# The gates and the second shift and scale of a diffusion layer: weighted sums of weight rows on the vector engine, with the matmul engine adding the 128 partial rows

## The chip, the cores and the metric

The kernel runs on one core of one Trainium2 chip. The engines are named as in the profile: PE is the matmul engine (PEld is its weight load, which overlaps its matmuls), DVE the vector engine, ACT the scalar engine, POOL GpSimd, SP the queue that issues most transfers. The metric is the device time of one execution in microseconds (us), the median of three runs; lower is better.

## The reference

The layer has adaLN modulation, two attentions in parallel (multi-head latent attention and 2-D neighbourhood attention over 512 latent and 256 context tokens), a gated residual, a router and 16 experts of which each token uses two. Only the first lines below are touched:

```python
def adaln(cond, w_mod, b_mod):
    return jnp.split(jax.nn.silu(cond) @ w_mod + b_mod, 6, axis=-1)
...
sh1, sc1, g1, sh2, sc2, g2 = [m[:, None, :] for m in adaln(c, w_mod[l], b_mod[l])]
hx = modulate(rmsnorm(x, norm_attn_g[l]), sh1, sc1)
...
x = x + g1 * mixed
hx2 = modulate(rmsnorm(x, norm_ffn_g[l]), sh2, sc2)
x = x + g2 * hierarchical_moe(hx2, ...)
```

`silu(c)` is one vector of 1024 numbers and `w_mod` is 1024 x 6144 in float32. The first 2048 columns (`sh1`, `sc1`) are wanted at once and are computed apart, early. The other 4096 columns (`g1`, `sh2`, `sc2`, `g2`) are one vector times 16 MB of weights, wanted only after the neighbourhood attention.

## The kernel before

All work is in float32, most of it as matmuls of a high and a low part: `mm3` issues three matmuls (lines 56, 57, 58), whose parts ACT (a copy to the short type) and DVE (the difference) make. The stages, in order of time: modulated norm and the projections (0 to 122 us); the neighbourhood attention (about 122 to 262 us); the latent attention (to about 390 us); output projection and router (to about 460 us); the experts and the last norm.

The change lies in the neighbourhood attention. Its loop (line 707) runs over 32 blocks: four pairs of heads, in each pair two heads of four row blocks. For a block, PE makes the scores (lines 599 and 600), DVE adds the bias (line 605, `na_max`) and takes the row maximum (line 469, `row_max`), ACT takes the exponentials (line 612), PE turns them (line 621, `na_turn`) one block later, and DVE and ACT in turn copy the turned block out (lines 81 and 83). Between these, PE projects the next pair's queries and keys (`na_project`, 24 `mm3` for a pair) or, in the last pair, the latent heads' values (`mla_values`); ACT and DVE split what PE made (lines 578 to 584) and the next pair's weights (lines 554 and 557). At a pair's end come the sums over values (line 630) and their normalisation (lines 479 to 490).

The four modulation vectors are computed in the same loop by `mod_rest` (line 509), called behind every second block, 16 times. Call n takes one tile of 128 rows of `w_mod` (k = n mod 8) and half of the columns (r = n // 8): two loads of 512 KB, then four matmuls with the 128 x 32 tile `sstat[:, k, :]` as the weights (column 0 is `silu(c)`, column 1 that of the context vector, the rest zeros) and 512 columns moving, each on its own 32 columns of PE (`tile_position`). The trace shows each of these float32 matmuls as two instructions, so eight for a call. Eight calls accumulate in one bank of the sums' memory; behind the eighth, DVE adds the bias row (line 524) and SP writes four rows of 512 to memory (line 525), from where `g1` (line 881), the router's weights (line 964), the second norm (lines 1069 and 1072) and `g2` (line 1331) read them.

The loads go by `load` (line 177) into tiles named `raw`, of which there are three. The same three tiles serve the weights of queries and keys (line 549, twice in a pair) and, in the last pair, seven loads for the latent attention (`mla_weights`, `mla_values`). All are issued in order on SP, and a load waits until its tile has been read to the end.

In this stage the order on each engine is written by a planner when the program is built: it goes by the program's order and its own estimates of durations, and lets later instructions go ahead of earlier ones that it takes to be not ready. On the chip each engine then keeps that order and waits where an operand is late. The experts' stage is ordered by hand.

Of the kernel before, what the change touches and what calls it, by code (L numbers as in the profile page):

```python
# [8 lines left out]
F32 = mybir.dt.float32  # L9
# [4 lines left out]
OP = mybir.AluOpType  # L14
# [3 lines left out]
P = 128  # L18
# [12 lines left out]
# columns of the constant pack  # L31
# [6 lines left out]
def hybrid_kernel(tc, nc, x_k, x_q, ctx, cvec, w_mod_a, w_mod_b, b_mod_c, b_mod_r, g_ffn_row,  # L38
# [25 lines left out]
    # low parts that wait for their turn on the vector engine  # L64
# [22 lines left out]
    def rstd_steps(out, ss, n, n_cols, wk, first=None):  # L87
        """1 / sqrt(ss / n + eps): the root of the scalar engine, and one Newton step on its inverse.
        Of a sum in two parts the first one comes earlier."""
# [25 lines left out]
    # ------------------------------------------------------------ constants and small parameters  # L115
# [31 lines left out]
    # ------------------------------------------------------------ pools of the first phases  # L147
# [4 lines left out]
    # the tokens come in the places of the attentions' results  # L152
# [12 lines left out]
    # the root's table, ahead of its use  # L165
# [35 lines left out]
    def bank(*nums):  # L201
        """A bank of the sums' memory, of those named in turn."""
        n = taken[nums] = taken.get(nums, -1) + 1
        return psA.tile([P, 512], F32, name="ps", tag=f"b{nums[n % len(nums)]}", bufs=1)
# [8 lines left out]
    # ------------------------------------------------------------ modulated norm of the tokens, channel-major  # L213
# [24 lines left out]
    def mod_sums(q):  # L238
        """Shift and scale of two channel tiles, for latent and context tokens."""
# [14 lines left out]
    def mod_first(c):  # L254
        """The same of one of the first two channel tiles."""
# [90 lines left out]
    # ------------------------------------------------------------ latents of keys and values, of queries  # L346
# [30 lines left out]
    # what leaves for the memory lies apart from what follows  # L377
# [49 lines left out]
    # ------------------------------------------------------------ ring of the experts' weights  # L427
# [17 lines left out]
    def load_experts(n, behind=None):  # L445
        """Starts the loads of the next n chunks of experts' weights, in the order of their use."""
        for i in range(len(loads), min(len(loads) + n, len(order))):
# [6 lines left out]
            # few in flight, so that the small transfers between them don't queue for long  # L454
# [7 lines left out]
    # ------------------------------------------------------------ neighbourhood attention  # L462
# [3 lines left out]
    def row_max(s):  # L466
        """A block's row maximum, negated."""
        nm = cst.tile([P, 1], F32, name="nm", tag="nm", bufs=8)
        ve.tensor_reduce(out=nm, in_=s, axis=AX.X, op=OP.max, negate=True)  # L469
        return nm  # L470

    def softmax_block(s, pr, ssum):
        """exp of a block of scores less their row maximum, and the row sums."""
        ac.activation(pr, s, AF.Exp, bias=row_max(s), accum_out=ssum)

    def normalise_steps(ssum, wk, hi, lo):
        """Divides a pair of heads' sums by their rows' sums, which are turned into rows on the way."""
# [21 lines left out]
    # the sums of the experts' rows, by tokens  # L499
# [4 lines left out]
    # the other modulations, as rows  # L504
    mod_d = tc.dram_tile([2, 4, 512], F32, name="mod_d")
    modf = mod_d.rearrange("r a b -> r (a b)")
    mod_ps = []

    def mod_rest(n):
        r, k = divmod(n, KT)  # L510
        if k == 0:
            br = nw.tile([P, 512], F32, name="br", tag="br", bufs=1)
# [3 lines left out]
            mod_ps[:] = bank(7), br, rows  # L516
        ps, br, rows = mod_ps
        ws = [load(w_mod_b[r, k, :, q * 1024:(q + 1) * 1024]) for q in range(2)]
        for g in range(4):
            pe.matmul(ps[g * 32:(g + 1) * 32, :], sstat[:, k, :],  # L520
                      ws[g // 2][:, g % 2 * 512:g % 2 * 512 + 512], start=(k == 0), stop=(k == KT - 1),
                      tile_position=(0, g * 32))
        if k == KT - 1:
            ve.tensor_tensor(br, br, ps, op=OP.add)
            sy.dma_start(mod_d[r], rows)
# [17 lines left out]
    def na_bias(p, u):  # L543
        """The bias of a head, with the window's mask."""
# [4 lines left out]
    def na_weights(p, j, i):  # L549
        """The high part (i = 0) and the low one (1) of the weights of queries (j = 0) or keys (1)."""  # L550
# [8 lines left out]
    def na_project(p, j):  # L559
        """Queries (j = 0), latent keys (1) or context's keys (2) of a pair of heads. Yields between the steps."""  # L560
# [9 lines left out]
    def na_part(p, j, u, i):  # L570
        """Their high part (i = 0) and low one (1), of a head."""
# [42 lines left out]
    def na_turn(p, u, i):  # L614
        """A block's weights by keys."""
# [32 lines left out]
    # ------------------------------------------------------------ latent attention  # L648
# [9 lines left out]
    def mla_values(t):  # L658
        """Values of the latent heads, and the queries' weights and latents in two parts. Yields between the steps."""
# [29 lines left out]
    for j in range(3):  # L689
        for n, _ in enumerate(na_project(0, j)):  # L690
# [4 lines left out]
            if n == 4 and j == 1:  # L695
                na_weights(1, 0, 0)
                na_weights(1, 0, 1)
                # the table of exp, ahead of its use
# [102 lines left out]
    def halves(n):  # L801
        """Two banks for sums of 1024 columns, by halves."""
# [11 lines left out]
    def k_rope(b):  # L814
        """The part of the keys that the heads share."""
        split_later(khs[b][64:96, :], kls[b][64:96, :], krt[64:96, :])

    def queries(a, ts=range(4)):
        """Queries of four heads."""
# [18 lines left out]
    def k_prep(p, hf):  # L838
        """Keys of a pair of heads, of the latent tokens (hf = 0) or the context's (1)."""
# [39 lines left out]
    # the neighbourhood heads' part of the output projection, between the pairs  # L879
# [55 lines left out]
    def mla_turn(h, t):  # L935
        """A block's weights by keys."""
# [22 lines left out]
    def router_weights():  # L959
        """The router's sums of the second shift, the same for all rows; then its weights take up the gains of the  # L960
# [937 lines left out]
```

## Time and profile before

| | |
|---|---|
| median of 3 runs | 760.02 us (759.91 to 760.87) |
| profiled execution, first to last instruction | 759.4 us |
| PE busy | 721.5 us, 95% of the span |
| DVE busy | 546.4 us, 72% |
| ACT busy | 446.0 us, 59% |
| mean granted TensorE clock | 0.980 |

The runs' median lies 0.6 us above the profiled span. Busy time is a sum over stages with different limits; a matmul's end is modelled in the profile, so how fast PE goes is better read from the starts of its instructions in order of time than from its busy share. A line such as "DVE L605 <- PE ps L600: 35.0" says that DVE stood idle for 35.0 us ahead of line 605 until line 600 on PE had ended.

### The profile page before, as it was taken

What the parts mean: (1) busy time and instruction counts of PE and PEld (TensorE: products, weight loads), DVE (VectorE), ACT (ScalarE), POOL (GpSimd) and SP (SyncE); (2) the same over time, 40 slices, a digit from 0 to 9 for tenths busy, and PEclk for the clock granted to TensorE, in tenths of its full rate; (3) what the DMA queues carried; (4) which work ended last, traced back from release to release, by engine and by line L of the source; (5) the groups of instructions that cost most, each with busy time, mean ns of one, the idle gap of its engine ahead of it and who ended that gap; (6) DMA issues with size and microseconds to landing.
All of it is one profiled execution on the core that took longest, in us unless ns stands there. A gap on an engine that the chain in (4) does not pass through costs nothing. (4 is left out here: it accounts for less than half of the span.)

```text
span 759.4 us, 10561 instructions
## 1 busy us (share of the span) xinstructions
PE 721.5 (95%) x3982; PEld 527.0 (69%) x3983; DVE 546.4 (72%) x744; ACT 446.0 (59%) x697; POOL 77.8 (10%) x46
## 2 busy tenths in 40 slices
PE   4999999999999999999999929999999999999995
PEld 4679987666665588776666826777777777777773
DVE  5572465646565589474564758999999999999996
ACT  6452364444434466464583428777777777777773
POOL 1000000000000000000000001033222322221220
PEclk9999999999999999999999958999999999999998
DMA  8931237544446662031139968999999999999872
GB/s 324 406 99 49 83 131 244 187 146 146 140 140 220 182 227 85 28 112 42 43 144 345 339 231 309 351 377 371 356 361 367 368 354 359 364 355 384 309 131 110
DMA packets 39621, 176.94 MB, mean 233 GB/s; under 512 B 5288, under 2 KB 6768, under 8 KB 27280
## 3 DMA queue, kind: packets, MB, share of 16 engines
q1 hardware_dynamic: 35168, 164.24, 58.6%
q0 software_dynamic: 4112, 11.92, 7.4%
q8 instruction: 32, 0.52, 0.3%
q14 instruction: 21, 0.17, 0.1%
q10 hardware_dynamic: 288, 0.08, 0.0%
HBM read 163.00 MB, written 15.32 MB: 235 GB/s over the span
## 5 line engine op out<-in xcount | busy, mean ns | idle before, releaser
L1356 DVE TENSOR_TENSOR el<-ew,eh 128x2048 fp32r<-128x2048 f32 (+1 forms) x106 | 220.5, 2087 | 20.7 <-ACT eh L1353 13.4
L1353 ACT CAST eh<-ew 128x1024 fp32r<-128x1024 f32 x190 | 189.7, 1048 | 43.2 <-PE s L58 28.6
L56 PE MATMUL s<-eh,xh 128*96 128x512 f32 x260 | 104.4, 401 | 0.9 <-ACT xh L61 0.9
L58 PE MATMUL s<-eh,xl 128*96 128x512 f32 x260 | 102.8, 396 | 0.0
L57 PE MATMUL s<-el,xh 128*96 128x512 f32 x260 | 102.4, 394 | 0.0
L1567 POOL DMA_INDIRECT ya_d<-yo,idx x14 | 45.5, 3253 | 140.4 <-DVE yo L1571 140.4
L58 PEld LDWEIGHTS s<-eh,xl 128*96 128x96 f32 x260 | 42.2, 162 | 19.1 <-DVE xl L62 0.6
L56 PEld LDWEIGHTS s<-eh,xh 128*96 128x96 f32 x260 | 42.2, 162 | 17.9 <-ACT xh L61 1.2
L57 PEld LDWEIGHTS s<-el,xh 128*96 128x96 f32 x260 | 42.3, 163 | 17.3 <-DVE el L1356 0.2
L56 PE MATMUL y<-eh,ghh 128*96 128x512 f32 x120 | 48.2, 401 | 0.0
L58 PE MATMUL y<-eh,ghl 128*96 128x512 f32 x120 | 47.3, 394 | 0.0
L57 PE MATMUL y<-el,ghh 128*96 128x512 f32 x120 | 47.2, 393 | 0.0
L56 PE MATMUL ps<-wh,hh 128*128 128x512 f32 (+2 forms) x128 | 43.8, 345 | 0.4 <-ACT hh L274 0.3
L469 DVE TENSOR_REDUCE nm<-s 128x1 f32<-128x768 f32 x32 | 30.5, 954 | 19.0 <-PE s L58 18.7
L58 PE MATMUL ps<-wh,hl 128*128 128x512 f32 (+2 forms) x128 | 43.5, 345 | 0.3 <-DVE hl L276 0.3
L57 PE MATMUL ps<-wl,hh 128*128 128x512 f32 (+2 forms) x128 | 43.3, 341 | 0.0
L1284 POOL MEMSET xg<- 128x1024 f32 x2 | 1.8, 950 | 388.0 <-DMA g<-mod_d 388.0
L605 DVE TENSOR_TENSOR ps<-ps,bb 128x256 f32<-128x256 f32 x32 | 13.8, 432 | 35.1 <-PE ps L600 35.0
L56 PE MATMUL ps<-hh,wh 128*128 128x512 f32 (+1 forms) x96 | 38.7, 403 | 0.0
L1242 POOL DMA_INDIRECT xg<-hx_d,idx x16 | 23.6, 1475 | 118.9 <-DVE va L1165 50.5
L933 ACT ACTIVATE pr<-s,nm 128x768 f32<-128x768 f32 x32 | 29.0, 908 | 9.6 <-DVE nm L469 9.3
L58 PE MATMUL ps<-hh,wl 128*128 128x512 f32 (+1 forms) x96 | 34.5, 359 | 0.0
(357 smaller groups left out, 1501.4 us busy)
## 6 DMA issues: line engine op xcount, KB each, us to landing
ew<-w_gate SPq DMA_DIRECT2D x32, 1024.0 KB, 9.3
ew<-w_up SPq DMA_DIRECT2D x32, 1024.0 KB, 9.2
ew<-w_down SPq DMA_DIRECT2D x32, 1024.0 KB, 9.3
raw<-w_mod_b SPq DMA_DIRECT2D x32, 512.0 KB, 3.8
wm<-w_mod_a SPq DMA_DIRECT2D x16, 512.0 KB, 9.2
raw<-w_qk SPq DMA_DIRECT2D x8, 512.0 KB
ya_d<-zero SPq DMA_DIRECT2D x10, 256.0 KB, 7.5
raw<-w_v SPq DMA_DIRECT2D x4, 512.0 KB
```

Source lines behind the costliest of these rows:

```text
L56: pe.matmul(ps, lh, rh, start=start, stop=False)
L57: pe.matmul(ps, lh, rl, start=False, stop=False)
L58: pe.matmul(ps, ll, rh, start=False, stop=stop)
L469: ve.tensor_reduce(out=nm, in_=s, axis=AX.X, op=OP.max, negate=True)
L605: ve.tensor_tensor(s[:, 0:256], s[:, 0:256], bb[:, 1 if i == 3 else 0, :], op=OP.add)
L933: ac.activation(pr, s, AF.Exp, bias=nm, accum_out=mla_ssum[h // 2][:, t, h % 2:h % 2 + 1])
L1242: ins = gp.indirect_dma_start(out=xg[e % NX][slice(0, CAP), :], out_offset=None, in_=hx_d, in_offset=bass.IndirectOffsetOnAxis(ap=idx[slic ...
L1284: gp.memset(x_, 0.0)
L1353: ac.copy(wh[:, cs], r[:, cs])
L1356: ve.tensor_tensor(wl[:, cs], r[:, cs], f(wh[:, cs]), op=OP.subtract)
L1567: gp.indirect_dma_start(out=ya_d, out_offset=bass.IndirectOffsetOnAxis(ap=idx[rows, 1, e:e + 1], axis=0), in_=yo[rows, :], in_offset=None, ...
```

## The change

`mod_rest` is rewritten, and the layout of its weights with it. The columns are now taken in eight pieces of 512 (r = n // 2), and each piece is finished by two calls, each of which takes four of the eight row tiles. For each row tile DVE multiplies the tile's 128 x 512 weights by `silu(c)` of the row (a scalar for each partition) and adds them to `macc`, a 128 x 512 tile. Behind the eighth row tile PE multiplies a 128 x 32 tile of ones by `macc`, 128 columns on each of its four strips, which adds the 128 rows; DVE adds the bias and SP writes a row of 512, eight times instead of two rows of 2048. The bytes loaded and the number and size of these loads (32 of 512 KB) are the same.

```diff
-    mod_d = tc.dram_tile([2, 4, 512], F32, name="mod_d")
-    modf = mod_d.rearrange("r a b -> r (a b)")
+    mod_d = tc.dram_tile([8, 4, P], F32, name="mod_d")
+    modf = mod_d.rearrange("(h r) a b -> h (r a b)", h=2)
     mod_ps = []
+    macc = nw.tile([P, 512], F32, name="macc")
+    ones = nw.tile([P, 32], F32, name="ones")
+    ve.memset(ones, 1.0)
 
     def mod_rest(n):
-        r, k = divmod(n, KT)
-        if k == 0:
-            br = nw.tile([P, 512], F32, name="br", tag="br", bufs=1)
+        r, h = divmod(n, 2)
+        if h == 0:
+            br = nw.tile([P, P], F32, name="br", tag="br", bufs=1)
             ve.memset(br, 0.0)
             rows = br.rearrange("(a b) n -> a b n", b=32)[:, 0, :]
             sy.dma_start(rows, b_mod_r[r])
-            mod_ps[:] = bank(7), br, rows
-        ps, br, rows = mod_ps
-        ws = [load(w_mod_b[r, k, :, q * 1024:(q + 1) * 1024]) for q in range(2)]
-        for g in range(4):
-            pe.matmul(ps[g * 32:(g + 1) * 32, :], sstat[:, k, :],
-                      ws[g // 2][:, g % 2 * 512:g % 2 * 512 + 512], start=(k == 0), stop=(k == KT - 1),
-                      tile_position=(0, g * 32))
-        if k == KT - 1:
-            ve.tensor_tensor(br, br, ps, op=OP.add)
+            mod_ps[:] = br, rows
+        br, rows = mod_ps
+        for k2 in (2 * h, 2 * h + 1):
+            w = load(w_mod_b[r, k2])
+            for i in range(2):
+                k = 2 * k2 + i
+                wk = w[:, i * 512:i * 512 + 512]
+                if k == 0:
+                    ve.tensor_scalar(macc, wk, sstat[:, k, 0:1], None, op0=OP.mult)
+                else:
+                    ve.scalar_tensor_tensor(macc, wk, sstat[:, k, 0:1], macc, op0=OP.mult, op1=OP.add)
+        if h:
+            ps = bank(7)
+            for g in range(4):
+                pe.matmul(ps[g * 32:(g + 1) * 32, 0:P], ones, macc[:, g * P:(g + 1) * P], start=True, stop=True,
+                          tile_position=(0, g * 32))
+            ve.tensor_tensor(br, br, ps[:, 0:P], op=OP.add)
             sy.dma_start(mod_d[r], rows)
...
-    a["w_mod_b"] = c(wm[:, 2048:].reshape(KT, P, 2, 2048).transpose(2, 0, 1, 3))
+    a["w_mod_b"] = c(wm[:, 2048:].reshape(4, 2, P, 8, 512).transpose(3, 0, 2, 1, 4).reshape(8, 4, P, 1024))
...
-    a["b_mod_r"] = c(bm[2048:].reshape(2, 4, 512))
+    a["b_mod_r"] = c(bm[2048:].reshape(8, 4, P))
```

## Rows read from the trace of the kernel before

**Rows 1.** Busy us by stretch, four pairs of heads: PE, PEld, DVE, ACT, POOL; clock, DMA

```profile
122.00:155.30 33.30, 33.30 (x172) 21.63 (x171) 19.60 (x35) 13.94 (x31) 0.00 (x0) 1.00 0.57 180
155.30:191.80 36.50, 36.50 (x213) 24.07 (x214) 20.22 (x36) 16.23 (x33) 0.00 (x0) 1.00 0.45 152
191.80:227.50 35.70, 35.70 (x208) 23.19 (x208) 19.99 (x36) 15.53 (x33) 0.00 (x0) 1.00 0.42 135
227.50:262.00 34.50, 34.50 (x182) 19.20 (x182) 20.24 (x36) 17.61 (x37) 0.00 (x0) 1.00 0.59 197
```

**Rows 2.** Waits in 122 to 262 us: total, times, longest

```profile
PEld ps L599 <- DVE pt L81: 0.8, 1, 0.8
```

**Rows 3.** PE in order of time, around one call and where none is; the group

```profile
134.91 0.60 PE L621 MATMUL ps<-c,pr 128*128 128x128 f32 x4
135.44 1.06 PE L520 MATMUL ps<-raw,sstat 128*32 128x512 f32 x8
136.44 0.50 PE L56 MATMUL ps<-hh,wh 128*128 128x512 f32 x1
...
176.29 0.60 PE L621 MATMUL ps<-c,pr 128*128 128x128 f32 x4
176.65 0.48 PE L56 MATMUL ps<-hh,wh 128*128 128x512 f32 x1
...
L520 PE MATMUL ps<-raw,sstat 128*32 128x512 f32 x128 | 20.2, 605 | 0.0
```

**Rows 4.** PE in order of time, a call in two parts

```profile
240.30 1.05 PE L520 MATMUL ps<-raw,sstat 128*32 128x512 f32 x4
241.29 0.50 PE L56 MATMUL ps<-wh,kvh 128*128 128x512 f32 x1
```

**Rows 5.** PE in order of time, 128-column matmuls of the first modulations

```profile
25.19 1.52 PE L245 MATMUL ps<-wm,sstat 128*32 128x128 f32 x48
...
42.39 0.42 PE L245 MATMUL ps<-wm,sstat 128*32 128x128 f32 x6
42.74 0.50 PE L56 MATMUL ps<-wh,hh 128*128 128x512 f32 x1
```

**Rows 6.** DVE groups by shape, 0 to 120 us: busy us, mean ns

```profile
L275 DVE SCALAR_TENSOR_TENSOR xnt<-xnt,ab,hh 128x576 f32<-128x576 f32 x8 | 6.4, 814 | 1.9 <-ACT hh L274 1.9
L276 DVE TENSOR_SCALAR hl<-xnt,ab 128x576 fp32r<-128x576 f32 x8 | 4.0, 515 | 0.1
L275 DVE SCALAR_TENSOR_TENSOR xnt<-xnt,ab,hh 128x256 f32<-128x256 f32 x8 | 3.8, 479 | 0.7 <-ACT hh L274 0.7
L276 DVE TENSOR_SCALAR hl<-xnt,ab 128x256 fp32r<-128x256 f32 x8 | 2.7, 349 | 0.1
```

**Rows 7.** DVE in order of time: a dependent pair, then two independent ones

```profile
126.19 0.43 DVE L605 TENSOR_TENSOR ps<-ps,bb 128x256 f32<-128x256 f32 x1 [1.05 <-PE ps L600]
126.66 1.29 DVE L469 TENSOR_REDUCE nm<-ps 128x1 f32<-128x512 f32 x2
```

**Rows 8.** DVE groups by shape, 122 to 290 us: the small steps

```profile
L833 DVE TENSOR_TENSOR q<-s,ckq 128x128 f32<-128x128 f32 x8 | 2.3, 286 | 0.7 <-ACT qt L832 0.7
...
L524 DVE TENSOR_TENSOR br<-br,ps 128x512 f32<-128x512 f32 x2 | 1.4, 689 | 1.7 <-PE ps L520 1.7
...
L513 DVE MEMSET br<- 128x512 f32 x1 | 0.5, 485 | 0.1
```

**Rows 9.** Busy us by stretch, in the experts' stage

```profile
520.00:700.00 180.00, 180.00 (x856) 128.02 (x855) 170.04 (x103) 138.52 (x154) 46.29 (x19) 1.00 1.02 364
```

**Rows 10.** DVE in order of time, end of the stage

```profile
259.81 0.69 DVE L524 TENSOR_TENSOR br<-br,ps 128x512 f32<-128x512 f32 x1 [1.43 <-PE ps L520]
260.42 0.68 DVE L81 COPY pt<-ps 128x512 f32<-128x512 f32 x1
```

**Rows 11.** SP's waits, 122 to 262 us; transfers issued 225 to 262 us

```profile
SPq L179 <- PE ps L520: 73.5, 19, 8.3
...
raw<-w_mod_b SPq DMA_DIRECT2D x8, 512.0 KB, 3.9
```

## The prediction

> **What bounds the kernel now.** I read the busy time by stretch first, then the waits, then PE in order of time. The change touches one stage, 122 to 262 us. [...] A busy PE alone proves little, since its ends are modelled; the waits say more. The longest time for which PE's weight load waited for another engine in these 140 us is one wait of 0.8 us [rows 2]. So PE sets the pace here, and a microsecond less on PE is one less of the stage as long as nothing else is late. DVE has 140 - 80.05 = 60 us of gaps (sum of the four stretches [rows 1]). What follows the stage hangs on it as a chain: the latent attention begins when the tiles and sums of this stage are given back, and the experts' loads begin behind it. I let it move by what the stage gains or loses, and keep 1 us either way for it in the range.
>
> **What is taken from PE.** One call shows as eight instructions of 605 ns, which does not mean 4.8 us: the four strips run side by side. From the turn ahead of it (134.91) to the matmul behind it (136.44) pass 1.53 us, and where no call stands between a turn and that matmul, 0.36 us (176.29 to 176.65); a call costs 1.17 us of PE [rows 3]. Thirteen of the sixteen calls are whole. The last three, all in the last pair, are cut in two because their two loads land apart, and each half costs 0.99 us (240.30 to 241.29), as much as a whole call less the change of tile [rows 4]. The group's 20.2 us busy are 19 pieces of 1.06 us, which agrees: 13 + 6 [rows 3]. Removed: 13 x 1.17 + 6 x 0.99 = 21.1 us; by pairs 4.7, 4.7, 4.7 and 7.1.
>
> **What PE gets instead.** Eight groups of four matmuls over 128 columns, two instructions each. The first modulations have the same form: in a long run 48 instructions take 1.52 us, so eight take 0.25 us; a short group of six takes 0.35 us from its start to the next matmul [rows 5]. I take 0.5 us, with bounds of 0.25 and the 0.99 of a half call [rows 4]: 4.0 us, 1.0 in each pair. PE then needs 33.3 - 3.7 = 29.6, 36.5 - 3.7 = 32.8, 35.7 - 3.7 = 32.0 and 34.5 - 6.1 = 28.4 us.
>
> **What DVE gets.** 64 new steps on 128 x 512: 56 multiply-adds with a scalar for each partition and 8 plain multiplications. Both forms stand in the first stage with 576 and 256 columns; between them, 512 columns make 479 + (814 - 479) x 256/320 = 747 ns and 349 + (515 - 349) x 256/320 = 482 ns [rows 6]. How far apart they start depends on whether they hang on one another: the maximum that reads what line 605 wrote starts 0.47 us after it, 0.04 more than it took; of two independent steps of 0.69 us the two together take 1.29, so they start 0.60 apart, 0.08 less than one takes [rows 7]. All eight sums of a piece hang on one another through `macc`, but other steps may stand between. Bounds: all dependent, 56 x 0.787 + 8 x 0.522 = 48.3 us; all hidden, 56 x 0.667 + 8 x 0.402 = 40.6 us. Neither row is nearer, since the planner will use part of the seams; I take the middle, 44.4. The small steps: eight adds of 128 columns at 0.286 for two of 0.689, +0.9 us; eight memsets of a quarter of the columns, at most 0.2 each, for two of 0.485, +0.6 at most, say +0.4 [rows 8]. Together 45.7 us, 11.4 in each pair.
>
> **The sum.** DVE then needs 31.0, 31.6, 31.4 and 31.6 us in the four pairs, against 29.6, 32.8, 32.0 and 28.4 on PE. So the two stand level, and in the first and last pair DVE is the longer. With both filled to the last gap the stage would take 31.0 + 32.8 + 32.0 + 31.6 = 127.4 us, 12.6 less. That will not happen: DVE keeps its order and has to wait for scores, exponentials and loads. The nearest stretch in which DVE is nearly full beside a PE that never stops is the experts', 170.04 of 180 us, a fill of 0.945 [rows 9]. At that fill the pairs take 32.8, 33.4, 33.2 and 33.4, 132.8 us, which is 7.2 less. The end of the stage gives some back: the last call's four sums, the ones and the add now stand where one add of 0.69 us stood, ahead of a copy that the last turn waits with [rows 10]. That is between nothing, if the sums are done while PE still projects, and 3 us, the four sums in a row; I take 1.5. Net 5.7 us less on the profiled span: 759.4 - 5.7 = 753.7, and with the 0.6 us by which the median lies above it 754.3 us.
>
> Edits that I cost at nothing: the loads are the same in number and size; six more writes of 2 KB and six more small loads of the bias go through SP, which in this stage waits 73.5 us for PE to give back the `raw` tiles [rows 11], so its own issue time is covered; the new rows are read only after the stage, and their writes are spread over it. If that cover were gone, a write or a load of the bias would delay the `raw` load behind it by its issue alone. New on DVE is a wait for loads. Before, the loads were PE's operands; now everything behind a sum in DVE's order (bias, maximum, then ACT's exponentials, then PE's turn) waits with it.
>
> [...] The rows give 0.47 us from start to start for a dependent pair whose first takes 0.43, and 0.60 for two independent ones of 0.69 [rows 7]. [...]
>
> **The rivals.**
> *DVE's chain is cheap.* If dependent sums start as close as independent ones, the added work is 40.6 + 1.3 = 41.9 us, 10.5 a pair, and DVE's pairs at the same fill take 31.9, 32.5, 32.3 and 32.5. PE's 32.8 counts in the second, so 129.5 us; with the 1.5 of the end, 9.0 less: 751.0 us. For it: other steps that stand between two sums hide the seam. Against it: four sums come at a time and hang on one another.
> *Everything packs.* 12.6 less and no loss at the end: 747.4 us. Against it: no stretch of the trace has DVE at 1.00.
> *The gain is eaten.* All sums at the dependent price: 49.6 us, 12.4 a pair, 32.0, 32.6, 32.4 and 32.6, at the fill of 0.945 together 137.2; with 3 us at the end the stage is as long as before, 760.2 us.
> *Slower: the three `raw` tiles hold the last pair.* There, 15 loads pass through three tiles (8 of the modulations [rows 11], 7 of the latent attention). A tile is held from its load's issue to its last reader: 3.9 us to land [rows 11], two sums (1.5 us), and the time for which it waits in DVE's order. The ring takes 15/3 = 5 holds, so it stays inside the pair's 33.4 us while a hold is under 6.7 us, a wait of 1.3 us. If each load waits behind a burst of four sums and one more step, 3.6 us, the hold is 9.0 and the pair takes 45 us where it took 34.5. Some loads are read by ACT and released earlier; with half of this excess the pair takes 39.2, the stage 138.6 and the end up to 3 us: 141.6, 1.6 slower; with all of it 144.4 + 3, 7.4 slower. I put it at the middle, 4.5 slower: 764.5 us. For it: the loads of this pair are late even now (the cut calls [rows 4]). Against it: the planner can place sums later when it sees the load late.
>
> **How the numbers follow.** Forecast 754.3 us with 0.45; the cheap chain 0.14; everything packs 0.06; eaten 0.12; slower 0.23. A measurement of this kernel can tell some 0.2%, 1.5 us, from no change. The first three are faster by more than that: 0.65; the fourth is the same: 0.12; the fifth slower: 0.23. The range for 8 in 10 reaches from everything packed, 747, to just under the slower rival's point, 764. The forecast's own range, with 0.25 to 0.99 us for the ones and 0 to 3 us at the end, is 751 to 758.
>
> **What would show it.** Right: line 520's successor on PE takes under 5 us in all; DVE is over 90% busy from 122 us to the stage's end; that end comes 4 to 8 us earlier; PE shows waits of about a microsecond for exponentials or for `macc`; the stages behind keep their lengths. The price of a sum is read from its row: 0.75 us each, 0.67 to 0.79 from start to start. Wrong: if DVE stays under 85% busy while PE waits, it is the order or the loads that hold, not DVE's work; if SP's waits for sums grow and ACT or DVE wait for `raw` in the last pair, it is the ring. If the stage's end moves and the kernel's does not, the later stages are not the plain chain that I take them for.

## The result, and the profile after

The changed kernel takes 764.97 us (median of 14 runs, 761.32 to 767.26) where the kernel before takes 759.79 on the same chip (14 runs, 757.49 to 761.76): a ratio of 1.0066, 95% interval 1.0051 to 1.0082. It is 5.2 us slower, where 5.7 us less were forecast, and 1 us above the range. The profiled execution went from 759.4 to 765.0 us and the mean granted clock from 0.980 to 0.960.

How long the touched stage takes is best read between two matmuls that stand in both kernels with the same work between them: the first projection of queries (`ps<-hh,wh`) and the first matmul of the latent attention (`o<-kvh,wkh`). Before they start at 104.06 and 265.24 us, after at 103.06 and 272.17: 161.2 and 169.1 us. From there to the end of the span pass 494.2 and 492.8 us. So the stage lost 7.9 us in these two executions and the stages behind kept their length. The change's profiled execution took 767.18 us, 2.2 more than its median, and its clock of 0.960 is the lowest of its 14 runs (median 0.967); the one of the kernel before took 759.91. So 7.9 us is more than the change costs in the middle. This stage length is used for all kernels below. (Some expectations quote how far the change stood ahead at the ends of the pairs, 3.7, 2.0, 0.7 and then 6.9 us behind, counted from the start of the span. The first projection itself starts up to 3 us apart in these executions; counted from there it is 2.7, 1.0, then 0.3 and 7.9 behind.)

The same stretches as [rows 1], and the rest of the stage, in the changed kernel (PE, PEld, DVE, ACT, POOL; clock, DMA):

```profile
122.00:155.30 33.30, 33.30 (x196) 24.09 (x194) 27.19 (x51) 15.16 (x33) 0.00 (x0) 1.00 0.61 199
155.30:191.80 36.50, 36.50 (x198) 25.81 (x192) 29.98 (x55) 16.00 (x33) 0.00 (x0) 1.00 0.45 153
191.80:227.50 35.70, 33.26 (x177) 22.38 (x175) 29.24 (x54) 15.05 (x32) 0.00 (x0) 0.90 0.42 137
227.50:262.00 34.50, 31.53 (x133) 19.49 (x129) 26.57 (x47) 13.97 (x30) 0.00 (x0) 0.75 0.53 171
262.00:272.20 10.20, 7.96 (x55) 5.66 (x55) 3.05 (x6) 2.59 (x6) 0.00 (x0) 0.67 0.52 175
```

The third column from the right is the news: the clock is granted in full for 70 us, then 0.90, 0.75 and 0.67 of it. DVE is fuller than before, but is busy for only 116.03 of these 150.2 us, and PE has gaps that it did not have. The waits of PE from 104 to 272 us (total, times, longest); in the kernel before PE has none to the stage's end at 265.24 us ([rows 2] shows its weight load, PEld):

```profile
PE ps L634 <- ACT pr L625: 2.2, 2, 1.4
PE ps L535 <- DVE macc L531: 2.1, 2, 1.2
PE ps L612 <- ACT pr L625: 1.7, 1, 1.7
PE ps L58 <- DVE wl L570: 1.2, 1, 1.2
PE ps L56 <- ACT wh L567: 0.5, 1, 0.5
```

Seven waits, 7.7 us. The groups that the change brought (line, engine, operation, tiles, shapes and count; busy, mean ns of one; idle before), DVE's four and PE's one:

```profile
L531 DVE SCALAR_TENSOR_TENSOR macc<-raw,sstat,macc 128x512 f32<-128x512 f32 x56 | 41.2, 735 | 0.1
L529 DVE TENSOR_SCALAR macc<-raw,sstat 128x512 f32<-128x512 f32 x8 | 3.7, 462 | 0.0
L537 DVE TENSOR_TENSOR br<-br,ps 128x128 f32<-128x128 f32 x8 | 2.3, 286 | 9.9 <-PE ps L535 9.9
L518 DVE MEMSET br<- 128x128 f32 x8 | 1.3, 165 | 0.0
...
L535 PE MATMUL ps<-macc,ones 128*32 128x128 f32 x64 | 3.9, 319 | 2.1 <-DVE macc L531 2.1
```

The prices are those of the forecast: 735 ns for a sum (747 from [rows 6]), 462 for a product (482), 0.49 us of PE for the ones (0.5). What the forecast has no line for is the 9.9 us that DVE stood ahead of the eight adds, until PE came to the ones.

**How a PE wait comes about.** DVE from the bias of one block (L618 at 233.15) to its row maximum (L469 at 240.38); columns are start, duration, line, operation, tiles:

```profile
233.15 0.43 DVE L618 TENSOR_TENSOR ps<-ps,bb 128x256 f32<-128x256 f32 x1 [1.24 <-PE ps L613]
233.49 0.68 DVE L62 TENSOR_TENSOR wl<-raw,wh 128x512 fp32r<-128x512 f32 x1
...
234.69 0.48 DVE L529 TENSOR_SCALAR macc<-raw,sstat 128x512 f32<-128x512 f32 x1
...
235.69 0.74 DVE L531 SCALAR_TENSOR_TENSOR macc<-raw,sstat,macc 128x512 f32<-128x512 f32 x1
...
236.49 0.73 DVE L531 SCALAR_TENSOR_TENSOR macc<-raw,sstat,macc 128x512 f32<-128x512 f32 x1
237.13 0.68 DVE L488 TENSOR_TENSOR rsb<-ps,rsb 128x512 f32<-128x512 f32 x1
237.73 0.74 DVE L531 SCALAR_TENSOR_TENSOR macc<-raw,sstat,macc 128x512 f32<-128x512 f32 x1
238.90 0.96 DVE L62 TENSOR_TENSOR uq<-raw,uq 128x768 fp32r<-128x768 f32 x1 [0.42 <-ACT uq L61]
239.78 0.68 DVE L490 TENSOR_TENSOR onl<-rsb,onh 128x512 fp32r<-128x512 f32 x1
240.38 0.68 DVE L469 TENSOR_REDUCE nm<-ps 128x1 f32<-128x512 f32 x1
```

The bias and the maximum that belong together stand 7.2 us apart. In the kernel before they are never more than 1.2 us apart in the last pair (2.0 in the whole stage); one of its blocks:

```profile
237.64 0.42 DVE L605 TENSOR_TENSOR ps<-ps,bb 128x256 f32<-128x256 f32 x1
...
238.84 0.68 DVE L469 TENSOR_REDUCE nm<-ps 128x1 f32<-128x512 f32 x1
```

Between the two steps of the changed kernel stand four steps of the sums, and copies and splits. ACT waits for that maximum, and PE for ACT's exponentials:

```profile
241.10 0.69 ACT L625 ACTIVATE pr<-ps,nm 128x512 f32<-128x512 f32 x1 [1.71 <-DVE nm L469]
...
241.93 0.38 PE L612 MATMUL ps<-kk,qh 128*128 128x256 f32 x1 [1.66 <-ACT pr L625]
```

**What comes behind it.** The stretches around PE's waits (the clock is the third number from the right):

```profile
200.00:210.00 10.00, 8.83 (x34) 6.49 (x34) 8.34 (x15) 4.83 (x11) 0.00 (x0) 0.83 0.46 146
220.00:230.00 10.00, 9.19 (x53) 5.33 (x51) 7.13 (x13) 4.72 (x10) 0.00 (x0) 0.83 0.69 222
240.00:245.00 5.00, 3.35 (x13) 1.96 (x11) 4.67 (x9) 2.39 (x5) 0.00 (x0) 0.86 0.49 168
245.00:260.00 15.00, 14.10 (x42) 8.40 (x42) 12.45 (x23) 5.03 (x11) 0.00 (x0) 0.50 0.60 194
260.00:265.00 5.00, 2.36 (x16) 1.66 (x18) 3.22 (x6) 2.78 (x6) 0.00 (x0) 0.84 0.23 77
265.00:270.00 5.00, 5.00 (x40) 3.79 (x42) 1.53 (x4) 0.62 (x1) 0.00 (x0) 0.50 0.78 245
```

From 245 to 260 us the granted clock is 0.50 without a break: matmuls of 512 columns start 0.43 us apart (256.98 to 257.41), where at 1.00 they start 0.23 us apart (237.12 to 237.35). The value sums of the last pair, 4.03 us long before (260.86), take 6.33 us here (265.49). Summed over these stretches, (1 - clock) x length is 1.7 + 1.7 + 0.7 + 7.5 + 0.8 + 2.5 = 14.9 us of matmul time not granted. The 2.2 us behind them, at a clock of 0.79, add 0.5. The sum is an upper bound of the cost, since PE also stood in some of this time.

**What no wait shows.** PE's new order also makes its own work longer. In the kernel before, the sums over values of the second pair stand in one run of 40:

```profile
192.94 3.72 PE L630 MATMUL ps<-pt,nav 128*64 128x512 f32 x40
```

In the changed kernel they stand in three pieces, one of two matmuls at 178.76 us and these, with the ones between them:

```profile
189.99 3.30 PE L643 MATMUL ps<-pt,nav 128*64 128x512 f32 x36
...
193.58 1.07 PE L643 MATMUL ps<-pt,nav 128*64 128x512 f32 x2
```

A piece of two takes a microsecond by itself and less than 0.2 within a run. From each piece's start to the start of what follows it, the value sums of the first three pairs take 11.9 us in 4 pieces before. In e4 (below), which issues the same 10 pieces for them as the change, they take 15.9 at the full clock and with no wait among them: 4.0 us more.

### The profile page after: what moved, and what is told of

Read it like the earlier page. It is cut to its first block, busy times and chain, and to the rows that moved or that the text cites. A ratio compares the mean times of both kernels' runs of the same rounds, so it can differ in the third digit from the quotient of the medians.

```text
span 765.0 us, 10562 instructions
## 1 busy us (share of the span) xinstructions
PE 720.5 (94%) x3918; PEld 533.3 (70%) x3919; DVE 584.4 (76%) x821; ACT 445.5 (58%) x697; POOL 77.7 (10%) x46
## 4 chain that ended last, share of the span: by engine, by line
PE 88%; DVE 5%; ACT 3%; DMA 3%; issue 1%; SPq 0%; DVEq 0%; ACTq 0%
PE s L56 11%; PE s L58 11%; PE s L57 11%; PE ps L56 6%; PE ps L58 6%; PE ps L57 6%; PE y L58 4%; PE y L56 4%; PE y L57 4%; PE ps L643 3%; PE o L968 3%; PE tr L959 3%; PE ps L613 2%; PE ps L634 2%; PE ps L612 2%; PE t L1511 1%
## 5 line engine op out<-in xcount | busy, mean ns | idle before, releaser
L469 DVE TENSOR_REDUCE nm<-s 128x1 f32<-128x768 f32 x32 | 30.5, 954 | 18.9 <-PE s L58 18.6
L531 DVE SCALAR_TENSOR_TENSOR macc<-raw,sstat,macc 128x512 f32<-128x512 f32 x56 | 41.2, 735 | 0.1
L625 ACT ACTIVATE pr<-ps,nm 128x512 f32<-128x512 f32 x32 | 22.0, 689 | 28.7 <-DVE nm L469 28.6
```

Of the source, the lines that this page charges most:

```text
L531: ve.scalar_tensor_tensor(macc, wk, sstat[:, k, 0:1], macc, op0=OP.mult, op1=OP.add)
```

## The experiments

All times are compared with runs of the kernel before on the same chip (medians 759.4 to 760.5). The kernels ran on several chips, so a difference of two of these medians is good to about a microsecond. "Pieces" are the eight of 512 columns, two to a pair of heads. Stage lengths come from one profiled execution each, from the first projection to the first latent matmul as above; that execution's own time stands beside them. The planner plans every kernel anew, so an edit can change the order on DVE and PE beyond its own lines.

| kernel | pieces on DVE | median us | ratio to before (95%) | profiled us | stage us |
|---|---|---|---|---|---|
| before | none, old layout | 759.79 | | 759.91 | 161.2 |
| the change | 0 to 7 | 764.97 | 1.0066 (1.0051 to 1.0082) | 767.18 | 169.1 |
| e1_late_add | 0 to 7, add one call later | 763.12 | 1.0040 (1.0016 to 1.0064) | 766.15 | 166.3 |
| e2_no_loads | 0 to 7, no loads for 6 and 7 | 761.40 | 1.0016 (0.9996 to 1.0036) | 761.25 | 164.8 |
| e3_filler | 0 to 7, matmuls added | 761.99 | 1.0031 (1.0015 to 1.0047) | 762.82 | 165.8 |
| e10_short_sums | 0 to 7, 6 and 7 of 64 columns | 755.08 | 0.9943 (0.9924 to 0.9961) | 753.48 | 156.5 |
| e7_pe_as_written | 0 to 7, PE's order as written | 782.87 | 1.0303 (1.0267 to 1.0340) | 782.80 | 183.3 |
| e6_only_last_dve | 6, 7 | 764.91 | 1.0052 (1.0026 to 1.0079) | 761.06 | 162.6 |
| e4_last_pe | 0 to 5 | 754.97 | 0.9924 (0.9900 to 0.9947) | 758.66 | 154.3 |
| e12_last_pe_late_add | 0 to 5, add one call later | 755.62 | 0.9944 (0.9926 to 0.9961) | 761.98 | 159.5 |
| e5_alt_pe | 0, 2, 4, 6 | 755.64 | 0.9950 (0.9927 to 0.9972) | 753.80 | 156.3 |
| e11_first_two_dve | 0 to 3 | 752.72 | 0.9917 (0.9891 to 0.9942) | 750.33 | 153.6 |
| e9_135_67_pe | 0, 2, 4 | 752.35 | 0.9887 (0.9852 to 0.9922) | 752.29 | 153.1 |
| e13_all_pe | none, new layout | 756.92 | 0.9973 (0.9960 to 0.9987) | 754.55 | 158.7 |

Many of the profiled executions lie far from their kernel's median, e6, e11 and e13 below it, e1, e4 and e12 above it. From the stage's end to the end of the span pass 492.2 to 494.9 us in all of them but e4 (498.3) and e12 (496.4); what these two took longer lies in part behind the stage.

Four theories stood at the start. The handshake: DVE stands 9.9 us ahead of the adds. DVE's queue: in the last pair bias and maximum come too late. The ring: the loads wait for one of three `raw` tiles, the slower rival of the prediction. The clock: PE's waits are short (1.7 us at most), but after them the granted clock is lower, 0.50 from 245 to 260 us.

**Put the add off (handshake).** The sum of the ones stays in its bank until the next call:

```diff
-            br = nw.tile([P, P], F32, name="br", tag="br", bufs=1)
+            br = nw.tile([P, P], F32, name="br", tag="br", bufs=2)
...
-            ve.tensor_tensor(br, br, ps[:, 0:P], op=OP.add)
-            sy.dma_start(mod_d[r], rows)
+            closing.append((br, rows, ps, r))
+        elif closing:
+            mod_close()
```

> The add of a piece's bias (line 537) and the write behind it are put one call later, eight times, so that the vector engine no longer stands before it until the matmul engine has come to the ones; all other work is the same. Theory A (the handshake between the two engines starts the loss: the vector engine stood 9.9 us before these adds, 3.3 us at each pair's end): the end of the attention stage, seen in the first matmuls behind the last transposed normalisation, comes from 271.8 us back to 262 to 266 and the kernel takes 755 to 759 us. Theory B (the vector engine is simply too full in the last pair): 762 to 766 us. Theory C (the three raw tiles): 762 to 766 us.

Measured: 763.12 us. The wait only moved. What DVE waited for from 104 to 272 us in this kernel (total, times, longest):

```profile
DVE macc L529 <- PE ps L535: 4.7, 3, 3.3
DVE rsb L488 <- PE ps L651: 4.3, 1, 4.3
DVE br L545 <- PE ps L535: 4.0, 1, 4.0
```

One of the first line's instances, in order of time:

```profile
193.49 0.48 DVE L529 TENSOR_SCALAR macc<-raw,sstat 128x512 f32<-128x512 f32 x1 [3.28 <-PE ps L535]
```

There is one `macc`, so the next piece's first product may not overwrite it before the ones have read it: the same PE instruction, the same 3.3 us. A second run of this edit without sums in the last pair (e12, below) gained nothing either. Taking the wait away altogether, with two `macc` tiles, was not tried.

**Take the loads of the last pair away (ring).** Pieces 6 and 7 read a tile that is there anyway, so they are not computed from their weights; all instructions of DVE and PE remain.

```diff
-            w = load(w_mod_b[r, k2])
+            w = load(w_mod_b[r, k2]) if r < 6 else nav[:, 2 * (k2 % 3):2 * (k2 % 3) + 2, :].rearrange("p a b -> p (a b)")
```

> In the last pair of heads the four calls make no loads: their sums read a tile that has lain in SBUF for long, so this part of the computation is left out in its meaning but not in its work on the vector and matmul engines. Theory C (three raw tiles hold the last pair, 15 loads through three of them): with 7 loads left the pair is free of them and the kernel takes 754 to 758 us. Theory B (the vector engine's work there): 762 to 766 us, since all sums are still made. Theory A (the handshake): 762 to 766 us.

Measured: 761.40 us, 3.6 less than the change, between the two ranges, and still not faster than before. The ring has a share; it is not the whole.

**Shorten the sums of the last pair, keep the loads (DVE's queue against the ring).** All loads, tiles, ones and writes stay; for pieces 6 and 7 only the first 64 columns are summed, the others are left out.

```diff
+                cols = 64 if r > 5 else 512
-                wk = w[:, i * 512:i * 512 + 512]
+                wk = w[:, i * 512:i * 512 + cols]
+                ma = macc[:, 0:cols]
```

> The changed kernel with the sums of the last pair (pieces 6 and 7) cut from 512 to 64 columns; the loads, their size, their tiles, the ones and the writes stay. The sums of the other columns of these two pieces are left out. The vector engine has some 16 x 0.6 = 10 us less to do in the last pair, the ring of raw tiles holds as many loads as before. If the vector engine's time is what makes this pair late, the pair takes what it takes with the sums on the matmul engine or less, and the time is 752 to 757 us. If the loads that wait for a tile make it late, little is gained: 761 to 765 us.

Measured: 755.08 us, 9.9 less than the change. Together with the run before it this shows which of the two leads. The ring carries as many loads as in the change, yet the whole loss of the last pair is gone (e4, below, has no sums there and takes as long). Short sums also give their tiles back sooner, so this run alone would not part the two; but with these loads out of the ring and the sums in full length (e2) 6.3 of the 9.9 us are still there. SP's longest wait for a sum to give a tile back, from 225 to 266 us, is 4.2 us in the change (total, times, longest):

```profile
SPq L179 <- DVE macc L531: 10.2, 6, 4.2
```

and here 1.2 us for a sum (L533), and 3.5 for a product (L531), once, at the pair's start:

```profile
SPq L179 <- DVE macc L533: 5.5, 8, 1.2
...
SPq L179 <- DVE macc L531: 3.5, 1, 3.5
```

So SP's waits alone don't tell DVE's queue and the ring apart; the times of e2 and e10 do.

**Only the last pair, and all but the last pair.** Pieces not on DVE are multiplied on PE in the new layout, four matmuls of 128 columns for each row tile; here for e4, with the list 0 to 5 for e6:

```diff
+        if r in (6, 7):
+            ps = mod_ps[2]
+            for k2 in (2 * h, 2 * h + 1):
+                w = load(w_mod_b[r, k2])
+                for i in range(2):
+                    k = 2 * k2 + i
+                    for g in range(4):
+                        o = i * 512 + g * P
+                        pe.matmul(ps[g * 32:(g + 1) * 32, 0:P], sstat[:, k, :], w[:, o:o + P],
+                                  start=(k == 0), stop=(k == KT - 1), tile_position=(0, g * 32))
```

> Pieces 0 to 5 (the first three pairs of heads) are summed on the vector engine as in the change; pieces 6 and 7 (the last pair) are multiplied and added on the matmul engine, four matmuls of 128 columns on each row tile. In the changed kernel the stage stood 3.7, 2.0 and 0.7 us ahead of the kernel before at the ends of the first three pairs and 6.9 us behind at the end of the fourth. If the loss belongs to the last pair alone (its sums, its three raw tiles, its waits), the stage's end comes 0.7 to 4.6 us before that of the kernel before: 755 to 759 us. If the loss comes from sums in all pairs alike, the clock falls in the last pair all the same and the time is 760 to 763 us.

> The complement: pieces 0 to 5 on the matmul engine, 6 and 7 on the vector engine. If the last pair itself cannot take the sums (the ring of raw tiles, or the vector engine's order in this pair), it loses there what the changed kernel lost in it, 7 us: 764 to 767 us. If the last pair only inherits a vector engine that is late from three pairs of sums, it starts here with nothing owed and the time is 756 to 761 us.

Measured: 754.97 us with the first three pairs on DVE, 764.91 us with the last alone. Two pieces in the last pair cost 4.4 us, nearly all that the change lost, with a DVE that owed nothing when the pair began; six pieces in the first three pairs gain 5.5 us, some 2.5 of which is the layout (e13, below).

The 7.2 us between a bias and its maximum are one way in which a full DVE stops PE, and not the measure of the loss. In the last pair the longest such distance is 3.6 us in e2, e3, e4 and e10, and 2.5 in e6, although e2 and e6 lose there and e4 and e10 do not. In the profiled execution of e6 PE waited 3.3 us at the ones for `macc` and 1.4 for exponentials.

**PE's order as written (planner).** The planner orders DVE and PE by its own estimates; one could blame it for the bias and maximum above.

```diff
+    kept = tc.manual_schedule(engines={pe.engine})
+    kept.__enter__()
     for b, (p, u, i) in enumerate(blocks):
```

> The changed kernel with the order of the matmul engine in this stage taken from the program as written instead of from the planner; all else alike. In the changed kernel the planner put scores, turns and value sums of the last pair one behind the other, with the projections in a bunch elsewhere, and the matmul engine stood for exponentials three times (1.4 to 1.7 us), after each of which the granted clock was at half. If that order makes the loss, the program's order, which sets a projection between scores and turn, gives 755 to 759 us. If the vector engine is simply too late with bias and maximum, the engine waits in this order too: 762 to 768 us.

Measured: 782.87 us, far above both ranges. In the written order PE comes to the ones before DVE has the last sum, and stands there (total, times, longest, 104 to 280 us):

```profile
PE ps L535 <- DVE macc L531: 20.7, 5, 5.1
```

So the planner had already moved the ones to where they cost 2.1 us. This run does not show that its order on DVE is the best one.

**Keep PE busy (clock).** Eight times in the last pair six unread matmuls of 512 columns:

```diff
+        if p == 3:
+            warm = bank(7)
+            for _ in range(6):
+                pe.matmul(warm, kvh[:, 0, 0:P], kvh[:, 0, 0:T], start=True, stop=True)
```

> Six matmuls of 512 columns that nobody reads are added to each of the eight blocks of the last pair, 48 in all, some 11 us of the matmul engine at full clock. Theory D (the clock: the granted clock is 0.50 between 245 and 260 us of the changed kernel, and the matmuls then take twice as long, which is worth up to 15 us): with the gaps filled the clock stays at 1.00 in the last pair and the kernel takes 756 to 763 us although it does more. Theory B (the vector engine sets the pace and the slow clock only fills time in which the matmul engine would wait): 764 to 770 us with the clock up. If the clock falls all the same: 768 to 778 us.

Measured: 761.99 us: 48 matmuls more, and 3 us less than the change. The stretch from 235 to 262 us, to compare with the clock of 0.50 from 245 to 260 in the change:

```profile
235.00:262.00 27.00, 27.00 (x130) 19.28 (x129) 22.64 (x41) 11.92 (x24) 0.00 (x0) 1.00 0.51 166
```

PE has no wait in this stretch and keeps the full clock. Some 11 us of added matmuls (48 x 0.23) cost less than the waits and the clock that they replace. But the planner's order on DVE is another one here too: a bias and its maximum are at most 3.6 us apart in the last pair, and PE waits 2.5 us in the whole stage instead of 7.7. So this run does not part the clock from the waits.

A second reading of the clock came unasked. From the normalisation's transposes (L485) of the second pair to those of the third, the change and e4 and e10 issue the same PE instructions and have the same three waits (0.5, 1.2 and 0.8 us). Their profiled executions differ in the clock alone. Stretch 198 to 235 us in e4, then in e10, then in the change:

```profile
198.00:235.00 37.00, 34.55 (x222) 22.83 (x220) 32.19 (x61) 18.48 (x40) 0.00 (x0) 1.00 0.49 159
```

```profile
198.00:235.00 37.00, 34.67 (x187) 23.24 (x187) 30.82 (x62) 17.20 (x38) 0.00 (x0) 0.95 0.50 160
```

```profile
198.00:235.00 37.00, 34.56 (x179) 22.82 (x179) 29.24 (x56) 17.39 (x37) 0.00 (x0) 0.91 0.45 149
```

The way from transposes to transposes takes 35.42, 36.99 and 38.56 us in them (195.84 to 231.26, 193.11 to 230.10, 194.58 to 233.14), and 39.78 us in e2, with the same instructions and a clock of 0.86. So the lower clock alone costs 3.1 us in this pair of the change against e4, near the bound of 3.4 that the two stretches of it above give, and nothing of it is DVE's time. PE in order of time behind the same wait, in e4 and then in the change:

```profile
202.97 0.50 PE L58 MATMUL ps<-hh,wl 128*128 128x512 f32 x1 [1.17 <-DVE wl L586]
...
204.01 0.39 PE L56 MATMUL ps<-hh,wh 128*128 128x512 f32 x1
204.24 0.40 PE L57 MATMUL ps<-hl,wh 128*128 128x512 f32 x1
```

```profile
201.71 0.50 PE L58 MATMUL ps<-hh,wl 128*128 128x512 f32 x1 [1.17 <-DVE wl L570]
...
202.79 0.63 PE L56 MATMUL ps<-hh,wh 128*128 128x512 f32 x1
203.21 0.63 PE L57 MATMUL ps<-hl,wh 128*128 128x512 f32 x1
```

512 columns start 0.23 us apart in the first and 0.42 in the second, a microsecond behind a wait of the same length.

**How many pieces, and where.** Three kernels share the pieces out otherwise, one has no sums on DVE, one puts off the add without sums in the last pair. The edits are the two above with other lists of pieces.

> Every second piece of 512 columns (1, 3, 5, 7) is summed by the matmul engine as before the change (64 instructions of 128 columns, some 2 us a piece), the other four by the vector engine. The matmul engine keeps about half of the 17 us that the change takes from it, the vector engine gets 5.7 instead of 11.4 us in each pair (a share of some 0.78). Theory B (too much work on the vector engine): no waits of over 1 us are left, the clock stays at 1.00 and the kernel takes 751 to 755 us. Theory A (the handshake, which four pieces still make): 756 to 760 us. Any theory by which sums on the vector engine cost at any amount: 760 to 763 us.

> As the kernel that alternates (pieces 1, 3, 5, 7 on the matmul engine, 755.6 us), with piece 6 on the matmul engine too, so that the last pair has no sums on the vector engine. If what is left of the loss there sits in the last pair (its clock was 0.87), the time falls to 752 to 755 us; if only the share of the work that left the matmul engine counts, it rises by about one piece, 2 us, to 757 to 758 us.

> Pieces 0 to 3 (the first two pairs) on the vector engine, 4 to 7 on the matmul engine: as many pieces on each as in the kernel that alternates (755.6 us). If any piece off the matmul engine is worth 2.1 us while nothing waits, four give 8 us at most and 752 to 755; the matmul engine had no wait in the first two pairs of the changed kernel. If the vector engine in a pair with two pieces gives part of this back later, by copies and splits that come late, 756 to 759.

> Pieces 0 to 5 on the vector engine, 6 and 7 on the matmul engine (755.0 us without the next edit), and the add behind the ones put off to the next call, so that the vector engine does not stand for the matmul engine there (9.9 us in all in the changed kernel). If this wait is a cost that is still paid with six pieces, 752 to 754 us. If it lies in time that the vector engine has to spare, 754 to 757 us.

> All eight pieces on the matmul engine in the new layout: the same loads, four matmuls of 128 columns on each row tile, no sums on the vector engine. It parts the layout from the vector engine's share. In the kernel before, the last three calls were cut in two, because their two loads land apart, which cost 6 x 0.99 us where whole calls cost 3 x 1.17, 2.4 us more; in the new layout a load holds two whole row tiles, and nothing is cut. If the layout alone gives this back, 757 to 758.5 us; if it does nothing, 759 to 761. The kernels with three and four pieces on the vector engine (752.4 and 752.7) are then 5 to 8 us better by the sums alone.

Measured: 755.64 us with every second piece, 752.35 when piece 6 goes to PE too: a single piece in the last pair costs 3.3 us (also by the stage; 4.2 when each is set against the kernel before on its chip) although it takes 1.9 off PE (two calls of 1.18 us, below, less 0.49 for the ones). With it PE waits 1.8 us at the ones and the clock is 0.87 from 235 to 262 us. 752.72 with the first two pairs whole, the same within the intervals; in this kernel the bias and maximum of a block of the last pair are again at most 1.2 us apart. 755.62 with the late add against 754.97 without: no gain. In that kernel's profiled execution (761.98) PE waited 3.5 us for exponentials and the clock was 0.86 from 198 to 235 us. All on PE in the new layout 756.92: the layout alone gives 2.5 us by the medians and by the stage (2.1 by the ratio), what the cut calls cost [rows 4]. Against the expectation two of the last calls are still cut; but a half now holds two whole row tiles on all four strips, where before it had two of the strips, and it costs 0.57 us (243.86 to 244.43) instead of 0.99:

```profile
243.86 0.65 PE L533 MATMUL ps<-raw,sstat 128*32 128x128 f32 x16
```

A whole call of four row tiles in e13, in order of time on PE:

```profile
132.57 0.60 PE L650 MATMUL ps<-c,pr 128*128 128x128 f32 x4
133.10 1.08 PE L533 MATMUL ps<-raw,sstat 128*32 128x128 f32 x32
134.11 0.50 PE L56 MATMUL ps<-hh,wh 128*128 128x512 f32 x1
```

From the turn to the projection pass 1.54 us, 0.36 without a call [rows 3], so a call costs 1.18 us and a piece on PE two of them.

So three or four pieces on DVE, none in the last pair, have the lowest medians: 8.1 and 7.0 us under those of the kernel before on their chips (the intervals of e4, e9 and e11 overlap). Some 2.5 of this is the layout, and the vector engine's help is worth the other 5.6 and 4.5. Four pieces gain no more than three since two full pairs cut the value sums: by the rule above these take 2.9 us more in e11 than in e13, and no more in e9.

## Why the prediction was wrong, step by step

**Right: what leaves PE and what it gets.** A call in the new layout costs PE 1.18 us (e13), as the 1.17 of [rows 3]; the ones take 3.9 us, as 4.0; and that cut calls cost more than whole ones [rows 4] is borne out by the 2.5 us that the layout alone gives. At these prices PE was relieved of some 17 us, as forecast.

**Right: DVE's price.** 44.9 us busy for the 64 steps; a sum starts 0.66 us ahead of the next step, since the planner put another step behind nearly all of them. That is the cheap end of the two prices, so the prediction's rival of the cheap chain was right in its cause. It did not decide. Without a step between, a dependence has its price here too: a product of 0.48 us and the sum that hangs on it start 0.52 us apart (155.77), 0.04 more than the first took, as in the dependent pair of [rows 7], while the independent steps there start 0.08 sooner than the first takes. The planner's order makes this matter little.

**Wrong: the fill.** The step that failed is the one that made pairs out of sums: "at that fill the pairs take 32.8, 33.4, 33.2 and 33.4". The fill of 0.945 came from the experts' stage [rows 9], which is ordered by hand. Here DVE was busy 27.19 of 33.3, 29.98 of 36.5, 29.24 of 35.7 and 26.57 of 34.5 us: 0.82, 0.82, 0.82 and 0.77. In the first two pairs PE had no wait and the full clock, so PE set the pace there still, and not DVE as the sum has it for the first. In the last two PE waited 7.7 us in all for steps of DVE and what hangs on them. The prediction named this itself as the sign that "it is the order or the loads that hold". A softmax block goes PE, DVE, ACT, PE; with two or three blocks in flight, a maximum that is 7 us late stops PE long before DVE is full. The gaps that [rows 1] shows on DVE were not all spare time: with them bias and maximum stood within 2.0 us in all pairs.

**Wrong: the adds priced by their duration.** The forecast has "eight adds of 128 columns at 0.286". Their operand comes from PE, and the planner places the ones behind value sums, so DVE stood 9.9 us. They should have been costed as a wait. But this wait does not explain the loss by itself: put off, it comes back at `macc`, and without sums in the last pair the kernel is fast with it (e4). What the kernel would take without it was not tried.

**Missing: the clock, and the price of PE's new order.** The prediction reckoned with the clock of 1.00 that [rows 1] show throughout. It said that PE would show "waits of about a microsecond" and charged nothing more for them. Those waits add up to 7.7 us and the matmul time not granted behind them to some 15 at most: 17 us less work on PE and 23 more would make the stage 6 us longer at most, where 7.9 were measured. The rest lies in a term that the prediction put at nothing, what the work left on PE costs in a new order: the value sums that are cut apart take 4.0 us more, and no wait shows it. With it the terms give at most 10 us. In e4 the clock is 1.00 from 198 to 235 us and its mean of 0.978 near the 0.980 of the kernel before, so the other terms can be added up: six pieces and the layout take 13.6 us off PE, the cut value sums give back 4.0 and the waits 2.4, so 7.2 us less; 6.9 were measured.

**The slower rival: right in place and size, wrong in mechanism.** It said the last pair, and 764.5 us, but its cause is another, so that the number comes so close is luck. It made the three `raw` tiles the cause. With all loads in the ring and the sums short the loss is gone (e10), with the ring relieved and the sums long only 3.6 of 9.9 us are gone (e2). So most of the loss is DVE's queue, and the ring has the smaller share. A load that waits "behind a burst of four sums" was put at 3.6 us; SP's longest wait for a sum in the last pair is 4.2.

**Where it is right: the chain behind.** The stages behind kept their lengths (494.2 and 492.8 us, and within 3 us of each other in all profiled executions but those of e4 and e12), and six more rows and bias loads on SP cost nothing that shows.

**Open.** Why the clock fell to 0.91 behind the same waits in one execution (the change, 198 to 235 us) and stayed at 1.00 in another (e4) was not settled. What two `macc` tiles or a DVE order with the sums behind every maximum would give in the last pair was not tried, and neither was an order on PE that keeps the value sums together.

## What to carry to other kernels

Gaps on an engine inside a chain of short, dependent steps over several engines are in part its response time, not all room for work (here 60 us of gaps on DVE, with bias and maximum within 2.0 us, and 7.2 us once sums stood in them): before filling them, look how far apart two steps that belong together already stand, and give work only to stretches in which the pacing engine does not yet wait. Where relief makes TensorE wait, count the granted clock behind the wait too (3.1 us in one pair of the change against e4), and price the work that stays on it in its new order: the value sums that are cut apart here cost 4.0 us more without any wait. Moving a part (here three or four of eight pieces, none in the fullest stretch) can win where moving all of it loses (752.4 and 752.7 us against 765.0).

## What the hardware showed that was not expected

- A wait of 1.17 us on TensorE, with one of 0.46 just before it, was followed in the change by matmuls of 512 columns that start 0.42 us apart at a granted clock of 0.50 (202.8 to 205.7), and in e4, with the same instructions, by none such: there they start 0.23 us apart. Four executions with the same instructions show a clock of 1.00 (e4), 0.95 (e10), 0.91 (the change) and 0.86 (e2) from 198 to 235 us. What sets it, and why it did not fall at all in e4, is not explained by any run.
- Adding work to the pacing engine made the changed kernel 3 us faster: 48 matmuls whose result nobody reads. The planner's order on DVE changed with them, and PE's waits fell from 7.7 to 2.5 us, so the clock is not shown to be the only reason.
- Two matmuls of a run of 40 take 1.07 us when they stand alone on PE between others (e4 and e11, at the full clock), and less than 0.2 us within the run (3.72 us for the 40 in the kernel before); the profile counts this as busy time.
